# Moving the indexer queries to their rows: one stacked product per head instead of two

## The chip, the cores and the metric

The kernel runs on one core of one Trainium2 chip. The metric is the device time of one execution in microseconds (us). TensorE (PE) multiplies, VectorE (DVE) and ScalarE (ACT) do elementwise work, GpSimd (POOL) does elementwise work and issues one kind of DMA, SyncE (SP) issues the others.

## The reference, cut to what matters

Two layers of an encoder, for 512 prompt frames and 64 sample frames (576 in all) with the same weights. In each layer an indexer with 8 heads of 32 numbers scores all keys, and attention then works on the best keys only:

```
qi = rope(qi.reshape(B, T, IDX_HEADS, IDX_DIM), pos)          # 8 heads x 32
ki = rope(ki[:, :, None, :], pos)[:, :, 0]
s = einsum('thd,sd->ths', qiB, kiB) * IDX_DIM ** -0.5
score = einsum('th,ths->ts', wB, relu(s)) * IDX_HEADS ** -0.5
_, sel = top_k(score, k_sel)
```

The selection has to agree with float32, so each float32 operand of an fp32r product is held as a high part (rounded to fp32r) and a low part (what is left).

## The kernel before, in words

Activations lie transposed: 128 features on partitions, 576 frames along the free axis. A projection of 128 output columns is one `block` (line 462): 8 steps (`step`, line 440) of 6 matmuls with 288 frames each, high and low parts of weights and activations, 48 matmuls into a PSUM buffer of the tag `mm` (2 buffers). All other PSUM use has the tag `sm` (4 buffers). DVE multiplies a block's result with the norm factor `Rt` and so empties the buffer.

Each layer begins with the two blocks of the indexer's queries (`ps_q0`, `ps_q1`), 4 heads in each; the blocks u, z, gate, k, q, v and more follow in the list `ORDER`. After rope a query block `qr` has four heads of 32 rows each on the 128 partitions. The scores want each head by itself as 128 rows [high, low, high, low] against the keys' rows `KS` = [high, high, low, low], so that one product with 128 rows gives the sum of the four partial products. `qi_out` (line 644) makes this: ACT copies the whole block to `h` (the high part), DVE subtracts to `lo`, and for each of the four heads m two products with 0/1 matrices (windows of `turn_m`) place the rows of `h` and of `lo` in one PSUM buffer, 448 frames (the first 128 need no scores). Two copies, by ACT for even m and by DVE for odd m, take the result to `QS` and `QSs`. `turn_m` is 544 columns behind `KS` in one buffer: POOL clears it, DVE writes eight 32x32 identities into it (lines 668 to 675).

The order of instructions is written out while the program is built. `Plan` (line 66) keeps an estimated clock for each engine and a ready time for each piece of data. Work other than blocks is in generators: `start` queues one with a rank (0 first), and `pump` (line 231), which is called after each step of six matmuls, runs those whose condition holds at the planned time. `need(engine, data)` is true when the data are ready by the plan, for PE 0.4 us before the planned time of PE (`MARGIN`); `psum_free` is true when an `sm` buffer is free by the plan. So a generator that isn't ready lets one more step of a block go ahead of it. Each engine then runs its instructions in the order written.

What follows in the code: `ki_stack` (line 688) splits the keys on ACT and DVE, PE transposes the head weights into an `sm` buffer and DVE copies them to `wcol`; `select` (line 738) computes scores and finds the best keys on DVE; `attend` (line 1126) and `sample` (line 1146) are attention for the prompt and sample frames, on PE, DVE and ACT, between the blocks; the layer ends with 12 blocks' worth of output products.

Of the kernel before, what the change touches and what calls it, by code (L numbers as in the profile page):

```python
# [10 lines left out]
F32 = mybir.dt.float32  # L11
F32R = mybir.dt.float32r
AF = mybir.ActivationFunctionType
OP = mybir.AluOpType

P = 128
# [3 lines left out]
T = TP + TS  # L20
# [45 lines left out]
class Plan:  # L66
# [142 lines left out]
    def need(self, eng, *aps, room=None):  # L209

        now, e = self.now, self.free[eng]
        if room is not None and e - now > room:
            return False
        t = max([self.ready(x, eng) for x in aps], default=0.0)
        return t <= (now - MARGIN if eng == "pe" else max(e, now) + EPS_T)

    def start(self, gen, rank=1):
        item = [rank, len(self.todo), gen, None]
        self.todo.append(item)
        self.todo.sort(key=lambda x: x[0])  # L220
        self.step(item)
        return item
# [46 lines left out]
def encoder_step(ctx: ExitStack, tc: tile.TileContext, a: dict):  # L269
    nc = tc.nc  # L270
    plan = Plan()
    pe, act, dve, pool, dma = (Engine(plan, n, e) for n, e in (
        ("pe", nc.tensor), ("act", nc.scalar), ("dve", nc.vector), ("pool", nc.gpsimd), ("dma", nc.sync)))
    need, start = plan.need, plan.start
# [10 lines left out]
    def tmp(n=T, dtype=F32):  # L285
        return rot.tile([P, 608], dtype, name="tmp", tag="tmp", bufs=NTMP)[:, :n]

    def quart(dtype=F32):
        plan.wait("quart", NQ)
        return plan.slot("quart", NQ, rot.tile([P, 2 * T], dtype, name="quart", tag="quart", bufs=NQ), True)  # L290
# [12 lines left out]
    def ps_mm():  # L303
        return plan.slot("mm", 2, psum.tile([P, 2, 512], F32, name="mm", tag="mm", bufs=2), False)

    def ps_s(hold=False):
        return plan.slot("sm", 4, psum.tile([P, 512], F32, name="sm", tag="sm", bufs=4), hold)
# [4 lines left out]
    def psum_free(k=1):  # L312
        return plan.slots("sm", 4, k)
# [122 lines left out]
    ps = ps_s()  # L436
# [25 lines left out]
    def block(xh, xl, nk=8):  # L462
        w, i = weights()
        split_to(i + 3)
        ps = ps_mm()
        product(ps, w, xh, xl, nk)
        return ps
# [90 lines left out]
    def layer(l, x, arrive):  # L558
# [24 lines left out]
        for k in range(8 + lag[1]):  # L583
# [4 lines left out]
            if k < 8:  # L588
                c = (k % 2) * T
# [17 lines left out]
        for s in range(2):  # L607
            c = slice(s * HT, (s + 1) * HT)
# [33 lines left out]
            return sh  # L642

        def qi_out(b, qr, sh):
            h, lo = tmp(dtype=F32R), tmp(dtype=F32R)
            dve.tensor_tensor(sh, sh, SI, op=OP.mult)
            dve.tensor_tensor(qr, qr, sh, op=OP.add)

            def go():
                yield lambda: need("act", qr)  # L650
                act.copy(h, qr)
                yield lambda: need("dve", h)
                dve.tensor_tensor(lo, qr, h.bitcast(F32), op=OP.subtract)

                for m in range(4):
                    yield lambda: psum_free() and need("pe", h, lo, turn_m)
                    ps = ps_s()
                    for i, s in enumerate((h, lo)):
                        c = 32 * (1 + 4 * m - i)
                        pe.matmul(ps[:, :T - P], lhsT=turn_m[:, c:c + P], rhs=s[:, P:T], start=i == 0, stop=i == 1)  # L660
                    copy = dve.tensor_copy if m % 2 else act.copy
                    copy(QSv[:, 4 * b + m], ps[:, :3 * P])
                    copy(QSsv[:, 4 * b + m], ps[:, 3 * P:T - P])
                done.add(("qi", b))

            start(go(), 0)

        KSW = quart(F32R)
        KS, turn_m = KSW[:, :T], KSW[:, T:T + 17 * 32]
        pool.memset(turn_m.bitcast(F32), 0.0)  # L670
        for m in range(4):
            r = slice(32 * m, 32 * m + 32)
            for i in (0, 2):
                c = 32 * (1 + 4 * m + i)
                dve.tensor_copy(turn_m[r, c:c + 32], ident[r, r])
        qi_out(0, qr0, sh0)

        ko = tmp()
# [46 lines left out]
        start(ki_stack(), 1)  # L725
        qr1 = tmp()
        qi_out(1, qr1, rope(ps_q1[:, :, :HT], qr1, CI, SI))

        macc = quart()
# [614 lines left out]
        for m2 in range(4):  # L1344
            w, n = weights()
            split_to(n + 3)
            for i in range(2):
                m = 2 * m2 + i
# [3 lines left out]
                ps = ps_mm()  # L1352
                product(ps, w, oh, ol, 4, off=512 * i)
                c = slice(i * T, (i + 1) * T)
# [25 lines left out]
        for m in range(8):  # L1380
# [7 lines left out]
            ps = block(mh, ml)  # L1388
# [57 lines left out]
        for s, t0, t1, starts in ((0, 0, CUT, (0, P, CUT - P)), (1, CUT, T, (CUT, T - P))):  # L1446
            for m in (6, 7):
                w, ps = wps[m - 6]
# [21 lines left out]
    def arrive(k):  # L1470
# [3 lines left out]
        if k == 1:  # L1474
            split_first()

    x = layer(0, x, arrive)
    for l in range(1, DEPTH):
        x = layer(l, x, lambda k: None)
# [106 lines left out]
```

## Time and profile before

| what | value |
|---|---|
| time, median of 3 runs | 921.59 us (921.48 to 923.78) |
| time of the profiled execution | 922.67 us |
| its span, first to last instruction | 920.9 us |
| PE busy | 895.8 us, 97% |
| DVE busy | 669.1 us, 73% |
| ACT busy | 593.3 us, 64% |
| POOL busy | 201.7 us, 22% |
| granted TensorE clock, share of full speed | 0.994 |

The profiled execution's own time is 1.8 us over its span and 1.1 us over the median. Busy time of an engine counts an instruction from its start to its end; matmuls overlap, so the distance between their starts tells what one costs in a row of them.

### The profile page before, as it was taken

How to read it: one execution, taken by the hardware profiler on the slowest of the kernel's cores; microseconds unless marked ns; L12 is line 12 of the kernel's file. 1: busy time of each engine (PE TensorE's matmuls, PEld its weight loads, DVE VectorE, ACT ScalarE, POOL GpSimd, SP SyncE). 2: the span in 40 equal slices, each digit the busy share in tenths (PEclk: the TensorE clock that was granted, in tenths of full speed). 3: DMA queues.
4: the chain of work that ended last, by engine and by line, in shares of the span. 5: the costliest groups of instructions: out<-in, count | busy, mean ns of one | idle time of the engine just before them, and what ended most of it. 6: DMA issues, size and time to landing. Idle time of an engine off the chain costs nothing.

```text
span 920.9 us, 17399 instructions
## 1 busy us (share of the span) xinstructions
PE 895.8 (97%) x6613; PEld 882.8 (96%) x6613; DVE 669.1 (73%) x1554; ACT 593.3 (64%) x1056; POOL 201.7 (22%) x217
## 2 busy tenths in 40 slices
PE   8999999999999999999999999999999999999995
PEld 7999999998999999999999999999999999999995
DVE  6896899799896676462259779988989875755314
ACT  7456533688898975564536564446889988556652
POOL 3111211135341310112210111113443222011121
PEclk9999999999999999999999999999999999999998
DMA  7757588766465775778976666787655558648862
GB/s 266 185 135 171 115 217 202 165 165 164 114 156 138 185 197 140 200 202 232 273 184 168 166 149 160 190 203 182 162 143 130 157 123 221 189 133 222 236 145 104
DMA packets 54500, 160.97 MB, mean 175 GB/s; under 512 B 6736, under 2 KB 9040, under 8 KB 54416
## 3 DMA queue, kind: packets, MB, share of 16 engines
q0 software_dynamic: 16416, 59.78, 34.7%
q1 hardware_dynamic: 38000, 100.08, 32.5%
q8 instruction: 52, 0.85, 0.4%
q14 instruction: 32, 0.26, 0.1%
HBM read 85.37 MB, written 14.69 MB: 109 GB/s over the span
## 4 chain that ended last, share of the span: by engine, by line
PE 67%; DVE 14%; ACT 14%; issue 3%; DMA 1%; POOL 1%; SPq 0%; DVEq 0%; ACTq 0%; POOLq 0%
PE mm L263 56%; PE sm L263 11%; DVE quart L263 6%; DVE tmp L263 6%; ACT prob L263 4%; ACT whl L263 3%; ACT quart L263 2%; ACT qz L263 1%; ACT L263 1%; ACT tmp L263 1%; DVE big L263 1%; POOL tmp L263 1%; DMA raw<-in_w_dram 1%; DVE acc L263 1%; DMA prob<-in_c_v_dram 1%
## 5 line engine op out<-in xcount | busy, mean ns | idle before, releaser
L263 PE MATMUL mm<-quart,whl 128*128 128x288 f32 (+1 forms) x5568 | 780.9, 296 | 1.2 <-DVE tmp L263 1.2
L263 PEld LDWEIGHTS mm<-quart,whl 128*128 128x128 f32 x5568 | 755.2, 188 | 3.3 <-ACT quart L263 1.5
L263 POOL DMA_DIRECT2D whl<-raw x114 | 99.1, 870 | 650.4 <-ACT whl L263 435.3
L263 ACT CAST whl<-raw 128x1024 fp32r<-128x1024 f32 (+1 forms) x118 | 121.8, 1033 | 130.3 <-PE mm L263 89.4
L263 ACT ACTIVATE whl<-raw 128x1024 fp32r<-128x1024 f32 x114 | 120.5, 1057 | 0.0
L263 ACT ACTIVATE prob<-prob,stat 128x128 f32<-128x128 f32 (+3 forms) x128 | 67.5, 554 | 6.8 <-DVE stat L263 6.4
L263 DVE SCALAR_TENSOR_TENSOR quart<-prob,wcol,quart 128x256 f32<-128x256 f32 (+4 forms) x60 | 42.1, 704 | 26.4 <-ACT prob L263 25.2
L263 ACT ACTIVATE prob<-sm 128x256 f32<-128x256 f32 (+4 forms) x72 | 33.6, 481 | 38.6 <-PE sm L263 38.6
L263 DVE MATCH_REPLACE8 quart<-stat,quart 128x256 f32<-128x256 f32 (+2 forms) x96 | 51.2, 540 | 0.0
L263 DVE MAX8 stat<-quart 128x8 f32<-128x256 f32 (+2 forms) x96 | 47.4, 542 | 0.0
L263 DVE MAX8 quart<-quart 128x8 f32<-128x544 f32 x64 | 46.2, 722 | 1.2
L263 DVE MATCH_REPLACE8 quart<-quart 128x544 f32<-128x544 f32 x64 | 45.4, 709 | 0.0
L263 DVE TENSOR_TENSOR tmp<-tmp 128x576 f32<-128x576 f32 (+7 forms) x62 | 44.3, 720 | 1.3
L263 DVE TENSOR_TENSOR quart<-quart 128x576 fp32r<-128x576 f32 (+6 forms) x30 | 26.4, 881 | 21.5 <-ACT quart L263 21.0
L263 DVE TENSOR_TENSOR big<-sm,big 128x512 fp32r<-128x512 f32 (+1 forms) x64 | 28.9, 483 | 16.3 <-ACT big L263 16.1
L263 ACT CAST quart<-tmp 64x512 fp32r<-64x512 f32 (+4 forms) x44 | 24.1, 566 | 21.8 <-POOL tmp L263 11.7
L263 ACT COPY prob<-sm 64x512 f32<-64x512 f32 (+1 forms) x24 | 12.3, 514 | 39.0 <-PE sm L263 38.6
L263 PE MATMUL sm<-quart,big 128*128 128x128 f32 (+3 forms) x176 | 32.1, 291 | 1.4 <-DVE tmp L263 1.4
L263 ACT CAST big<-sm 128x512 fp32r<-128x512 f32 (+2 forms) x72 | 28.0, 434 | 7.9 <-PE sm L263 7.4
L263 DVE CUSTOM_DVE_ANT_0 prob<-sm,quart 128x512 f32<-128x512 f32 (+2 forms) x48 | 25.8, 549 | 4.8 <-PE sm L263 4.8
L263 DVE SCALAR_TENSOR_TENSOR quart<-tmp,gains,quart 128x576 fp32r<-128x576 f32 x8 | 6.6, 820 | 29.4 <-ACT quart L263 29.4
L263 DVE TENSOR_TENSOR quart<-mm,tmp 128x576 f32<-128x576 f32 (+2 forms) x10 | 6.4, 638 | 29.0 <-PE mm L263 28.9
(157 smaller groups left out, 1028.4 us busy)
## 6 DMA issues: line engine op xcount, KB each, us to landing
raw<-in_w_dram SPq DMA_DIRECT2D x116, 512.0 KB, 4.6
whl<-raw POOLq DMA_DIRECT2D x114, 512.0 KB, 4.9
mp<-tmp SPq DMA_DIRECT2D x16, 288.0 KB, 3.1
tmp<-mp SPq DMA_DIRECT2D x16, 288.0 KB, 4.8
prob<-in_c_k_dram SPq DMA_DIRECT2D x16, 256.0 KB, 5.0
prob<-in_c_v_dram SPq DMA_DIRECT2D x16, 256.0 KB, 3.8
out_o_v_dram<-quart SPq DMA_DIRECT2D x8, 320.0 KB, 4.5
quart<-in_x_dram SPq DMA_DIRECT2D x8, 288.0 KB, 6.3
```

What stands on the lines that cost most here:

```text
L263: return f(*args, **kw)
```

## The change

`qi_out` builds two operands per block instead of `h` and `lo`: `hl[e]` has the high parts of heads 2e and 2e+1 on its partitions 0 to 63 and their low parts on 64 to 127, 448 frames. ACT and DVE make each with one copy and one subtraction on 64 partitions. One product with a 0/1 matrix then moves a head's high and low rows, and `turn_m` is one 128x128 matrix for even heads and one for odd heads. The four instructions that make the operands are written out together, without a wait of the planner between a copy and its subtraction; a head's product waits for its own pair's operand.

```diff
         def qi_out(b, qr, sh):
-            h, lo = tmp(dtype=F32R), tmp(dtype=F32R)
+            hl = [tmp(dtype=F32R)[:, :T - P] for _ in range(2)]
...
             def go():
+
                 yield lambda: need("act", qr)
-                act.copy(h, qr)
-                yield lambda: need("dve", h)
-                dve.tensor_tensor(lo, qr, h.bitcast(F32), op=OP.subtract)
+                for e in range(2):
+                    src = qr[64 * e:64 * e + 64, P:T]
+                    act.copy(hl[e][0:64], src)
+                    dve.tensor_tensor(hl[e][64:128], src, hl[e][0:64].bitcast(F32), op=OP.subtract)
 
                 for m in range(4):
-                    yield lambda: psum_free() and need("pe", h, lo, turn_m)
+                    yield lambda: psum_free() and need("pe", hl[m // 2], turn_m)
                     ps = ps_s()
-                    for i, s in enumerate((h, lo)):
-                        c = 32 * (1 + 4 * m - i)
-                        pe.matmul(ps[:, :T - P], lhsT=turn_m[:, c:c + P], rhs=s[:, P:T], start=i == 0, stop=i == 1)
+                    pe.matmul(ps[:, :T - P], lhsT=turn_m[:, (m % 2) * P:(m % 2 + 1) * P], rhs=hl[m // 2], start=True, stop=True)
...
-        KS, turn_m = KSW[:, :T], KSW[:, T:T + 17 * 32]
+        KS, turn_m = KSW[:, :T], KSW[:, T:T + 2 * P]
...
-                c = 32 * (1 + 4 * m + i)
+                c = P * (m % 2) + 32 * (i + m // 2)
```

## Rows read from the trace of the kernel before

**Rows 1.** The page, busy time and share of the span of each engine.
```profile
PE 895.8 (97%) x6613; PEld 882.8 (96%) x6613; DVE 669.1 (73%) x1554; ACT 593.3 (64%) x1056; POOL 201.7 (22%) x217
```

**Rows 2.** The page, chain that ended last: share of the span by engine.
```profile
PE 67%; DVE 14%; ACT 14%; issue 3%; DMA 1%; POOL 1%; SPq 0%; DVEq 0%; ACTq 0%; POOLq 0%
```

**Rows 3.** Stretches of the span: length, then each engine's busy time, clock, DMA share, GB/s.
```profile
38.90:47.20 8.30, 8.30 (x54) 8.05 (x55) 8.02 (x20) 5.57 (x15) 0.99 (x2) 1.00 0.88 256
184.00:322.00 138.00, 135.84 (x1004) 132.77 (x1002) 115.37 (x296) 120.21 (x250) 50.51 (x47) 1.00 0.60 153
322.00:377.00 55.00, 52.97 (x401) 52.21 (x402) 36.76 (x89) 33.02 (x61) 5.17 (x6) 1.00 0.64 167
377.00:460.00 83.00, 83.00 (x624) 82.93 (x623) 32.55 (x47) 48.07 (x62) 16.57 (x17) 1.00 0.87 234
```

**Rows 4.** PE in order of time, first layer: start, length, operation, [idle before, releaser].
```profile
42.14 1.79 PE L263 MATMUL sm<-tmp,quart 128*128 128x448 f32 x8
43.77 1.76 PE L263 MATMUL mm<-quart,whl 128*128 128x288 f32 x12
45.36 1.79 PE L263 MATMUL sm<-tmp,quart 128*128 128x448 f32 x8
46.99 7.36 PE L263 MATMUL mm<-quart,whl 128*128 128x288 f32 x54
```

**Rows 5.** The same for the second layer.
```profile
488.61 1.38 PE L263 MATMUL sm<-tmp,quart 128*128 128x448 f32 x6
490.37 0.64 PE L263 MATMUL sm<-tmp,quart 128*128 128x448 f32 x2 [0.38 <-DVE wcol L263]
490.85 1.75 PE L263 MATMUL mm<-quart,whl 128*128 128x288 f32 x12
```

**Rows 6.** Groups by shape: busy us, mean ns of one, idle before.
```profile
L263 ACT CAST qz<-tmp 64x512 fp32r<-64x512 f32 x32 | 19.8, 620 | 4.0 <-DVE tmp L263 3.5
L263 ACT COPY quart<-quart 64x256 f32<-64x256 f32 x4 | 1.6, 404 | 0.1
L263 DVE TENSOR_TENSOR qzl<-tmp,qz 64x512 fp32r<-64x512 f32 x16 | 10.9, 683 | 0.3
L263 DVE TENSOR_TENSOR prob<-sm,prob 64x256 f32<-64x256 f32 x8 | 3.3, 417 | 12.4 <-ACT prob L263 12.4
L263 ACT ACT_TABLE_LOAD x17 | 21.8, 1283 | 1.0 <-PEq L1560 0.7
```

**Rows 7.** All engines in order of time, first layer: the instructions that split and read.
```profile
37.44 0.67 ACT L263 CAST tmp<-tmp 128x576 fp32r<-128x576 f32 x1 [3.96 <-DVE tmp L263]
38.65 2.20 DVE L263 TENSOR_TENSOR tmp<-tmp 128x576 f32<-128x576 f32 x3
42.41 0.54 DVE L263 TENSOR_SCALAR wcol<-sm 128x24 f32<-128x24 f32 x3
43.78 0.75 DVE L263 TENSOR_TENSOR tmp<-tmp 128x576 fp32r<-128x576 f32 x1
```

**Rows 8.** DVE in order of time, second layer.
```profile
485.93 2.20 DVE L263 TENSOR_TENSOR tmp<-tmp 128x576 f32<-128x576 f32 x3
489.69 0.54 DVE L263 TENSOR_SCALAR wcol<-sm 128x24 f32<-128x24 f32 x3
```

**Rows 9.** POOL and DVE in order of time, first layer: clearing and filling `turn_m`.
```profile
25.44 0.89 POOL L263 MEMSET quart<- 128x544 f32 x1
30.98 1.07 DVE L263 CAST quart<-ident 32x32 fp32r<-32x32 f32 x8
```

**Rows 10.** PE in order of time: two idle times between 184 and 345 us.
```profile
221.10 0.77 PE L263 MATMUL sm<-ident,tmp 128*128 128x128 f32 x5 [0.89 <-ACT tmp L263]
337.37 0.63 PE L263 MATMUL sm<-ident,quart 128*128 128x128 f32 x4 [1.20 <-DVE quart L263]
```

**Rows 11.** DVE and PE in order of time, where the first layer's attention ends.
```profile
379.39 0.29 DVE L263 TENSOR_TENSOR quart<-prob,quart 128x128 fp32r<-128x128 f32 x1 [0.86 <-ACT quart L263]
376.70 15.54 PE L263 MATMUL mm<-quart,whl 128*128 128x288 f32 x115
```

## The prediction, before the kernel was run

> **What bounds the kernel now.** I read the page's busy times first: PE is busy 97% of the span, DVE 73%, ACT 64% [rows 1]. Then the chain that ended last: PE has 67% of it, DVE and ACT 14% each [rows 2], so time taken from PE should count, unless it falls where the chain runs through the other two. Then the stretches. Where the change sits, 38.9 to 47.2 us in the first layer, PE is busy 8.30 us of 8.30 and DVE 8.02: both are full, ACT (5.57) has room [rows 3]. In the attention of that layer (184 to 322 us) PE is busy 135.84 of 138.00 us with ACT at 120.21 and DVE at 115.37; to its end at 377 us PE has 52.97 of 55.00, and in the output products 83.00 of 83.00 [rows 3]. PE has work nearly everywhere, because a generator that isn't ready lets a step of a block pass. The granted clock is 1.00 in all these stretches [rows 3], the upper of the two levels, 2.4 GHz; as the stretch stays full I cost nothing for the clock. Last I read the instructions around the change in order of time, PE first, then who feeds it.
>
> **Removed from PE.** A query block has 8 products of 448 columns, two blocks in each of two layers make 32, and the change leaves 16. Their price is the distance between starts, not their length: the eight at 42.14 are followed by the next matmul at 43.77, the eight at 45.36 by one at 46.99, 1.63 us both times, so 1.63 / 8 = 0.204 us each [rows 4]. The second layer's first group takes 488.61 to 490.85 with 0.38 us of waiting in it [rows 5]; its product itself is no dearer, so I use 0.204. Removed: 16 x 0.204 = 3.26 us. That the remaining products have other data in their rows is no cost that a row shows: shape, type and the weights of 128 columns stay.
>
> The Trainium skill, in "TensorE: Matmul & The Clock Gate", section "Back-to-back issue gap", says that in a stream of weight load and matmul pairs the spacing is set by both together, and gives about 131 ns for 512 columns. An estimate by that page is 16 x 0.131 = 2.1 us removed in place of 3.26. The trace does not agree with 131 ns: the 448 columns here are 0.204 us apart [rows 4], and I stay with the row; what the page's price would bring is a rival below.
>
> **ACT and DVE.** Four copies of 128x576 at 0.67 us and four subtractions at 0.75 us [rows 7] become eight of each on 64x448. The trace has no such shape in this place, so I take it between two: ACT needs 620 ns for 64x512 and 404 for 64x256, 0.84 ns per column, so 620 - 54 = 566 ns for 448; DVE 683 and 417 ns, 1.04 ns per column, so 683 - 67 = 617 ns [rows 6]. Half the partitions save next to nothing. One block costs ACT 2 x 0.566 - 0.67 = +0.46 us and DVE 2 x 0.617 - 0.75 = +0.48 us; in all ACT +1.9 us and DVE +1.9 us (bounds from the two sizes: 404 to 620 gives ACT +0.6 to +2.3 us, 417 to 683 gives DVE +0.3 to +2.5 us). On ACT this is hidden by its room in the stretch. On DVE it delays what stands behind: the two subtractions of the keys, the copies of `wcol`, the emptying of block u and the second block's subtractions. Emptying u 0.5 us later costs nothing, as its PSUM buffer is wanted again only after the block in progress.
>
> The planner's wait between copy and subtraction goes, so DVE, which takes its queue in order, could now stand before a subtraction until ACT has copied. It does not get there early: in the first layer ACT's copy began at 37.44 and DVE finishes the two rope instructions ahead of the subtraction (two of the three in the group at 38.65) at about 38.65 + 2 x 0.73 = 40.1 [rows 7]; two copies end at 37.44 + 1.13 = 38.6. I cost this wait at 0; without that 1.5 us of cover it would be at most one copy, 0.57 us, per block.
>
> **When are the operands ready?** First layer, first block: DVE 40.1 + 1.23 = 41.3, PE asks at 42.14 [rows 4]: in time by 0.8 us. Second block: its subtraction began at 43.78 [rows 7], now 0.48 later, so the pair is ready at 44.9 and 45.5. PE, with its second group shifted as below, asks for them at 45.4 and 45.8. In time, by only 0.3 us for the second.
>
> **A wait that grows.** Four `sm` buffers serve four heads, and one of them holds the head weights until DVE has copied them to `wcol`. In the second layer the fourth head already waits for that: `wcol` ends at 489.69 + 0.54 = 490.23 [rows 8], the matmuls go on at 490.37 [rows 5]. With half the products PE asks 0.6 us sooner, and DVE is done 0.48 us later, at 490.71. By the code the planner then finds no free buffer and puts one step of six matmuls (half of 45.36 - 43.77, 0.80 us [rows 4]) ahead of the fourth head. PE asks at 488.61 + 3 x 0.204 + 0.80 = 490.02 and starts at 490.71 + 0.14 = 490.85: 0.83 us idle in place of 0.38, +0.45. In the first layer `wcol` ends at 42.41 + 0.54 + 0.48 = 43.43 [rows 7], so 43.57 against PE at 42.14 + 0.61 + 0.80 = 43.55: 0.02. Together +0.5. If no step comes between it is 1.25 + 0.82 = 2.1 us; if two do, the 0.38 of now goes as well. Bounds -0.4 to +2.1; I take +0.5. Behind the waiting matmul only PE's own steps stand, and DVE and ACT have work.
>
> **POOL.** It clears 256 columns in place of 544. The clearing ended at 25.44 + 0.89 = 26.33, DVE's first use is at 30.98 [rows 9]: 4.6 us of cover, worth nothing. The eight identities stay, as do the number of `tmp` buffers and all DMAs.
>
> **Sum.** -3.26 + 0.5 = -2.8 us. The profiled execution took 922.67 us, 1.8 over its span of 920.9, so 919.9 for one like it; against the median of 921.59 it is 918.8 us. Does the gain last to the end? In each layer PE would reach the attention 1.4 us earlier. Attention ends on PE with a stream of 115 matmuls from 376.70; the last operand for the output products is written at 379.39 + 0.29 = 379.7 [rows 11], while PE works on the last block for some 6.4 us (48 matmuls at 0.133 us, from 1.59 / 12). That is over 3 us of slack: 1.4 us fit in.
>
> **Rivals.**
> The attention is paced by ACT and DVE, and PE just waits longer there. For: the chain's 28% on these two [rows 2] and waits such as 0.89 us for ACT and 1.20 us for DVE [rows 10]. Against: PE idles only 2.16 us in 138. Price: the whole gain; 921.6, up to 923.5 if DVE's 1.9 us came on top.
>
> Slower: everything after the change is written in a new order, since planned times shift. If the gates' sigmoids and the exponentials then alternate once more in each layer, ACT loads its tables two more times each, 4 x 1.28 us [rows 6] = 5.1 us. If PE waits for ACT in that place, as it does at 221 us [rows 10], its own saving is lost too: 921.6 + 5.1 = 926.7. It decides only if both pairs land on such a wait; by half of it, 2.6 us, the result would be no visible change. Against: ACT has 138.0 - 120.2 = 17.8 us free there [rows 3].
>
> The new order loses waits: the two of [rows 10] come to 2.1 us and each layer has its own; without most of them 2.8 + 3 = 5.8 us are gained, 915.8.
>
> The change doesn't bring what it says: matmuls are removed that cost less than their distance. At the skill's price it is -2.1 + 0.5 = -1.6 us, 920.0.
>
> **How the numbers follow.** A measurement of this kernel can tell about 0.3%, 2.8 us, from no change, and my forecast lies on that edge. Forecast case 0.60 (918.0 to 920.4 by the bounds of the wait: 3.26 + 0.4 and 3.26 - 2.1), split 0.33 faster and 0.27 within; paced by others 0.14, within; slower order 0.14; waits lost 0.09, faster; cheap products 0.03, within. Faster 0.42, same 0.44, slower 0.14. The range that leaves out about 2 in 10, most of the slower order and the far end of the lost waits, is 916.0 to 924.0.
>
> **What would show it.** 16 products of 448 columns in groups 0.2 us apart, with 3.3 us less of them; eight copies near 0.57 us and eight subtractions near 0.62 us; a step of six matmuls between the third and fourth head of the first block; 0.8 us idle before that head in the second layer; after that PE's idle per layer as now. I am wrong if the stretches from 184 to 377 us take longer by as much as was saved before them, if table loads are more than 17, or if subtractions that read two partition ranges take much over 0.7 us.

## The result, and the profile after

| what | before | after |
|---|---|---|
| median, 6 runs each | 922.78 us (921.48 to 923.78) | 927.63 us (927.10 to 929.28) |
| profiled execution, its span | 922.67, 920.9 us | 927.59, 925.8 us |

The ratio of after to before is 1.0055, 95% interval 1.0045 to 1.0065: slower by 4.9 us, where 2.8 us of gain were forecast. The page shows less work on PE and nearly the same share [rows 1], and PE has more of the chain [rows 2]:

```profile
PE 894.0 (97%) x6597; PEld 881.2 (95%) x6597; DVE 676.4 (73%) x1558; ACT 594.8 (64%) x1060; POOL 201.2 (22%) x217
...
PE 74%; DVE 11%; ACT 11%; issue 2%; DMA 1%; POOL 1%; SPq 0%; DVEq 0%; POOLq 0%; ACTq 0%
```

Around the change, PE after in order of time, both layers (the lines that answer to [rows 4, 5]):

```profile
41.52 0.77 PE L263 MATMUL sm<-tmp,quart 128*128 128x448 f32 x3
42.14 0.96 PE L263 MATMUL mm<-quart,whl 128*128 128x288 f32 x6
43.18 0.44 PE L263 MATMUL sm<-tmp,quart 128*128 128x448 f32 x1
43.46 1.75 PE L263 MATMUL mm<-quart,whl 128*128 128x288 f32 x12
...
46.03 0.47 PE L263 MATMUL sm<-tmp,quart 128*128 128x448 f32 x1 [0.41 <-DVE quart L263]
...
490.93 0.45 PE L263 MATMUL sm<-tmp,quart 128*128 128x448 f32 x1 [0.91 <-DVE wcol L263]
```

The step of six matmuls stands between the third and fourth head, and the fourth waits 0.91 us for `wcol` in layer 1. By shape, after, the new copies and subtractions, and one group that the change doesn't touch (busy us, mean ns of one):

```profile
L263 DVE TENSOR_TENSOR quart<-quart 64x544 f32<-64x544 f32 x4 | 8.9, 2229 | 1.7 <-ACT quart L263 1.6
...
L263 DVE TENSOR_TENSOR tmp<-tmp 64x448 fp32r<-64x448 f32 x8 | 5.0, 619 | 0.2
...
L263 ACT CAST tmp<-tmp 64x448 fp32r<-64x448 f32 x8 | 4.5, 560 | 8.6 <-DVE tmp L263 8.5
```

The first group is two additions per layer that join two parts of the sample's scores ahead of its selection. The kernel before took 2.9 us for it, not 8.9:

```profile
L263 DVE TENSOR_TENSOR quart<-quart 64x544 f32<-64x544 f32 x4 | 2.9, 720 | 0.2
```

Where did the time go? I compared the same event in both traces. The matmul stream behind the first layer's attention begins at 376.60 after and 376.70 before. But after was 0.62 us ahead when the first query block's products came near (the 24 matmuls in front of them start at 38.25 against 38.87), so from there to the attention's end the first layer took 0.5 us longer, with the 1.6 us of its products saved. Most of the loss is in the second layer (layer 1). PE before:

```profile
642.83 0.40 PE L263 MATMUL sm<-quart,qz 128*128 128x512 f32 x1
770.70 0.33 PE L263 MATMUL sm<-ident,prob 128*128 128x128 f32 x1 [0.81 <-ACT prob L263]
785.39 0.63 PE L263 MATMUL sm<-ident,quart 128*128 128x128 f32 x4 [1.20 <-DVE quart L263]
824.72 15.54 PE L263 MATMUL mm<-quart,whl 128*128 128x288 f32 x115
```

and after:

```profile
644.93 1.33 PE L263 MATMUL sm<-ident,tmp 128*128 128x128 f32 x5 [2.92 <-ACT tmp L263]
645.91 0.78 PE L263 MATMUL sm<-quart,qz 128*128 128x512 f32 x1
766.12 0.44 PE L263 MATMUL sm<-ident,prob 128*128 128x128 f32 x2 [1.02 <-ACT prob L263]
774.39 0.40 PE L263 MATMUL sm<-ident,prob 128*128 128x128 f32 x1 [2.00 <-ACT prob L263]
790.61 0.63 PE L263 MATMUL sm<-ident,quart 128*128 128x128 f32 x4 [1.20 <-DVE quart L263]
829.95 10.34 PE L263 MATMUL mm<-quart,whl 128*128 128x288 f32 x76
```

The attention's first product is 3.1 us late (645.91 against 642.83), the last unit 3.7 (774.39 against 770.70), the sample's first transposes 5.2 (790.61 against 785.39), and so it stays. Behind both long waits the granted clock is at the lower level, 1.2 GHz, for some 3 us (stretches of after; the clock is the third figure from the right):

```profile
645.00:648.00 3.00, 3.00 (x11) 2.81 (x12) 1.94 (x6) 3.00 (x7) 0.69 (x1) 0.50 0.00 0
775.00:778.00 3.00, 3.00 (x14) 2.91 (x13) 1.05 (x2) 1.82 (x3) 0.00 (x0) 0.51 0.84 203
```

Why does the attention start late? DVE before, just ahead of it, in order of time:

```profile
627.42 1.47 DVE L263 TENSOR_TENSOR quart<-quart 64x544 f32<-64x544 f32 x2
...
630.40 0.81 DVE L263 STREAM_SHUFFLE tmp<-mm 128x576 f32<-128x576 f32 x1
...
636.39 0.82 DVE L263 STREAM_SHUFFLE tmp<-mm 128x576 f32<-128x576 f32 x1
```

DVE after:

```profile
628.68 0.83 DVE L263 STREAM_SHUFFLE tmp<-mm 128x576 f32<-128x576 f32 x1
...
630.73 4.48 DVE L263 TENSOR_TENSOR quart<-quart 64x544 f32<-64x544 f32 x2 [0.59 <-ACT quart L263]
...
638.31 0.81 DVE L263 STREAM_SHUFFLE tmp<-mm 128x576 f32<-128x576 f32 x1
```

POOL after:

```profile
630.99 1.76 POOL L263 TENSOR_TENSOR tmp<-tmp,St 128x576 f32<-128x576 f32 x1
632.83 1.80 POOL L263 TENSOR_TENSOR tmp<-tmp 128x576 f32<-128x576 f32 x1
```

The first shuffle is the key rope's, the last the first query rope's, from which ACT makes the operands `qz`. Behind these casts ACT copies the value block (at 644.25 after, 642.48 before), and for that copy PE's first value transposes wait. Before, the additions ran ahead of the key rope. After, they stand behind it, beside POOL's half of that rope, and take 4.48 us in place of 1.47; two selection rounds (MAX8, MATCH_REPLACE8) follow, and the query rope starts 1.9 us later although its block ended no later on PE.

### The profile page after: what moved, and what is told of

It is laid out like the page before. It is cut to its first block, busy times and chain, and to the rows that moved or that the text cites. A ratio compares the mean times of both kernels' runs of the same rounds, so it can differ in the third digit from the quotient of the medians.

```text
span 925.8 us, 17394 instructions
## 1 busy us (share of the span) xinstructions
PE 894.0 (97%) x6597; PEld 881.2 (95%) x6597; DVE 676.4 (73%) x1558; ACT 594.8 (64%) x1060; POOL 201.2 (22%) x217
## 3 DMA queue, kind: packets, MB, share of 16 engines
HBM read 85.37 MB, written 14.69 MB: 108 GB/s over the span
## 4 chain that ended last, share of the span: by engine, by line
PE 74%; DVE 11%; ACT 11%; issue 2%; DMA 1%; POOL 1%; SPq 0%; DVEq 0%; POOLq 0%; ACTq 0%
PE mm L263 63%; PE sm L263 12%; DVE quart L263 5%; DVE tmp L263 4%; ACT whl L263 3%; ACT prob L263 3%; ACT quart L263 2%; ACT qz L263 1%; DMA raw<-in_w_dram 1%; ACT tmp L263 1%; POOL tmp L263 1%; ACT big L263 1%; DVE acc L263 1%; DVE big L263 0%; ACT L263 0%
## 5 line engine op out<-in xcount | busy, mean ns | idle before, releaser
L263 ACT ACTIVATE prob<-prob,stat 128x512 f32<-128x512 f32 (+3 forms) x128 | 68.0, 555 | 4.3 <-DVE stat L263 3.9
L263 DVE TENSOR_TENSOR quart<-quart 128x576 fp32r<-128x576 f32 (+6 forms) x30 | 32.4, 1081 | 14.4 <-ACT quart L263 13.1
L263 PE MATMUL sm<-ident,prob 128*128 128x128 f32 x160 | 24.9, 277 | 5.9 <-ACT prob L263 4.4
L263 DVE TENSOR_TENSOR tmp<-mm,tmp 128x576 f32<-128x576 f32 x28 | 21.0, 751 | 12.2 <-PE mm L263 11.9
```

Source lines behind the costliest of these rows:

```text
L263: return f(*args, **kw)
```

## The experiments

Times are compared by the ratio to the kernel before on the same chip, in brackets its 95% interval; after stands at 1.0055. Traces of the same instructions reach layer 1 up to 1.2 us apart: its second query rope starts at 484.42 us in after and at 485.65 in `casts_behind_last_exp`, which is the same up to there. Where that matters, times in layer 1 are counted from this rope (484.57 in before).

**1. Operands or order?** `new_ops_old_order` writes the changed instructions in the order of before on every engine: the planner is charged for the old ones.

```diff
-                    act.copy(hl[e][0:64], src)
+                plan.run("act", "copy", (h, qr), {})
+                for e in range(2):
+                    nc.scalar.copy(hl[e][0:64], src[e])
...
+                        plan.run("pe", "matmul", ...)   # twice
+                    nc.tensor.matmul(..., rhs=hl[m // 2], ...)
```

> The changed kernel's instructions (stacked operands, 16 products) written in exactly the order of the kernel before: the planner is charged for the old ones. Theory 'order': the loss came from the new order of all later work, so here the change's own value shows, 3.3 us less of products less some 1 to 2 us of growing waits for the wcol buffer: 1 to 2.5 us faster than before, about 921 us. Rival 'operands': the stacked instructions themselves are dearer than thought (subtractions over two partition ranges, buffers freed late); then most of the loss stays with the old order: 926 to 928 us.

Measured: 922.75 us, ratio 0.9993 [0.9984, 1.0001]. The loss is gone, but so is the gain; PE's idle times at the products say why:

```profile
43.32 0.44 PE L666 MATMUL sm<-tmp,quart 128*128 128x448 f32 x1 [0.91 <-DVE wcol L263]
46.25 0.67 PE L666 MATMUL sm<-tmp,quart 128*128 128x448 f32 x2 [0.48 <-ACT quart L263]
...
491.05 0.45 PE L666 MATMUL sm<-tmp,quart 128*128 128x448 f32 x1 [1.71 <-DVE wcol L263]
493.97 0.68 PE L666 MATMUL sm<-tmp,quart 128*128 128x448 f32 x2 [0.48 <-ACT quart L263]
```

3.58 us, against 0.38 before: the 3.26 us saved are waited away.

`old_ops_new_order` is the reverse: the planner is charged for the new instructions, and the old ones are issued.

```diff
+                    plan.run("act", "copy", (hl[e][0:64], src), {})
+                    plan.run("dve", "tensor_tensor", (hl[e][64:128], ...), ...)
+                nc.scalar.copy(h, qr)
+                nc.vector.tensor_tensor(lo, qr, h.bitcast(F32), op=OP.subtract)
...
+                    plan.run("pe", "matmul", ...)   # once, two are issued
```

> The kernel before's instructions (h and lo, 32 products) written in exactly the order of the changed kernel. Theory 'order': as slow as the changed kernel or slower by the products, 927 to 931 us. Rival 'operands': as fast as the kernel before, 921 to 924 us.

Measured: 927.85 us, 1.0045 [1.0033, 1.0057], with the additions and waits of after:

```profile
645.26 1.33 PE L263 MATMUL sm<-ident,tmp 128*128 128x128 f32 x5 [2.93 <-ACT tmp L263]
766.42 0.44 PE L263 MATMUL sm<-ident,prob 128*128 128x128 f32 x2 [1.02 <-ACT prob L263]
774.69 0.37 PE L263 MATMUL sm<-ident,prob 128*128 128x128 f32 x1 [2.02 <-ACT prob L263]
```

So the order makes the loss. The stacked operands add nothing that can be told apart (1.0055 and 1.0045, with overlapping intervals), and in this order the 16 products that they save bring no visible gain either.

**2. Is it this order, or any other?** `old_ops_third_order` is before, with only the planner's PE clock set back after each query block.

```diff
+                plan.free["pe"] -= 0.82
                 done.add(("qi", b))
```

> The kernel before with all its instructions, only the planner's estimate of PE's clock set back by 0.82 us after each of the four query blocks, so that the later work is written in a third order. Theory 'order is chance': the time moves by some us in either direction with no instruction changed, 917 to 930 us and not within 1 us of the kernel before. Rival 'only this order': 921.5 to 924 us.

Measured: 928.5 us, 1.0047 [1.0034, 1.0059]. The same pattern, now in the first layer:

```profile
197.44 0.77 PE L263 MATMUL sm<-ident,tmp 128*128 128x128 f32 x5 [2.90 <-ACT tmp L263]
...
326.90 0.33 PE L263 MATMUL sm<-ident,prob 128*128 128x128 f32 x1 [2.02 <-ACT prob L263]
```

0.82 us in the planner's clock at each of four blocks, with no instruction changed, costs as much as the change. One more order doesn't tell what an order costs on average; whether the order of before is an unusually good one is not tested.

**3. The lower clock.** `fill_idle` is after with dummy products, whose results are overwritten, put into the two waits of layer 1.

```diff
+                for _ in range(12 if l == 1 and p == 0 else 0):
+                    nc.tensor.matmul(pv[:, :P], lhsT=ident, rhs=ident, start=True, stop=True)
...
+            for _ in range(7 if (l, p, e, j) == (1, 3, 1, 0) else 0):
```

> The changed kernel with dummy products in the two longest idle times of PE in the second layer (12 ahead of the first v transposes, 7 ahead of the last head's probability transposes); they compute nothing that is used. Theory 'clock': the granted clock was 0.50 for 3 to 4 us after each of these two idle times, which costs about 1.8 us each; with PE kept busy it stays at 1.00 and the time falls to 924 to 925 us. Rival: the idle time alone is the loss; no change, 927 to 928 us, or slower if the dummies get in the way.

Measured: 926.26 us, 1.0030 [1.0019, 1.0041]. The granted clock is 1.00 behind both places (644 to 650 and 774 to 779 us). Layer 1 gained 1.5 us, all of it behind the second: at the first, PE waits 0.69 us for ACT soon behind it (648.87), and the attention is no earlier at 766 us (281.7 us behind that layer's second query rope, as in after). The trace of `casts_behind_last_exp` (experiment 5) says the same: there the clock stayed at 1.00 behind a first wait of 2.93 us, and this event again comes 281.7 us behind the rope. So the lower clock is a part of the loss behind the second wait, and none that reaches 766 us behind the first.

**4. The late start: rounds or additions?** `rounds_behind_rope` is after, with DVE's two selection rounds of layer 1 held back behind the first query rope.

```diff
+                for k in range(8):
+                    step(ps, w, xh, xl, k, 8)
+                    if k == HOLD: holding[0] = True   # max, match_replace go to `held`
...
                 dve.tensor_tensor(qr, qr, sh, op=OP.add)
+                holding[0] = False
+                while held: ...   # issued here
```

> The changed kernel with one move on VectorE alone, in layer 1: the two selection rounds (MAX8 and MATCH_REPLACE8, 2 x 1.5 us) that stand between the sample's two 64x544 additions and the first query rope go behind that rope. Theory 'the attention of layer 1 starts late because VectorE is still at its selection when the first query block ends': the rope's shuffle starts at 635.6 to 636.0 in place of 638.31, the first query product at 643.0 to 643.5 in place of 645.91, TensorE's wait at 644.93 falls from 2.92 to under 1.3 us and no half clock follows it; all later events of layer 1 come 2.4 to 3 us earlier and the time is 924.6 to 925.4. Rival 'the half clock behind the wait and the ACT order later in the layer make the loss': the first wait shrinks, but the stretch to 766 us takes longer by as much, time 927 to 928.

Measured: 925.36 us, 1.0034 [1.0021, 1.0046]. The rope starts at 635.43 and the wait is 0.77 us, but of the 2 us gained there 1 is left at 766 us (765.27 against 766.12, in a trace that reached layer 1 0.18 us later): the held rounds now stand ahead of the subtractions that make `qzl`, and two new waits of 0.83 and 0.72 us follow. The rest of the gain is the clock behind the second wait, which was not lowered in this execution:

```profile
642.96 0.77 PE L263 MATMUL sm<-ident,tmp 128*128 128x128 f32 x5 [0.77 <-ACT tmp L263]
644.79 0.51 PE L263 MATMUL sm<-quart,qzl 128*128 128x512 f32 x1 [0.83 <-DVE qzl L263]
667.25 0.55 PE L263 MATMUL sm<-ident,prob 128*128 128x128 f32 x3 [0.72 <-ACT prob L263]
765.27 0.44 PE L263 MATMUL sm<-ident,prob 128*128 128x128 f32 x2 [1.02 <-ACT prob L263]
773.55 0.33 PE L263 MATMUL sm<-ident,prob 128*128 128x128 f32 x1 [2.02 <-ACT prob L263]
788.24 0.63 PE L263 MATMUL sm<-ident,quart 128*128 128x128 f32 x4 [1.20 <-DVE quart L263]
```

`adds_ahead_of_key_rope` is after, with DVE's two additions put ahead of the key rope, in both layers.

```diff
+                behind("dve", "stream_shuffle", (halves(sh), ps[:, :, :HT], SHUF), {})
+                behind("dve", "tensor_tensor", (halves(kr), ...), {"op": OP.mult})
...      # kept in `late`, with POOL's two, until the additions are out
             dve.tensor_tensor(s2[64:128], ...)
+            for eng, op, args, kw in late: ...
```

> The changed kernel with one move on VectorE and none elsewhere, in both layers: the two 64x544 additions of the sample go ahead of the first key rope's shuffle and product, so that they no longer run beside GpSimd's two 128x576 operations of that rope. In the traces so far the two additions took 1.47 us where GpSimd was idle (the kernel before, both layers) and 4.48 us where they ran beside these operations (the changed kernel, both layers). Theory 'VectorE's additions, both inputs in SBUF, stand still while GpSimd reads SBUF': they take 1.47 us again, GpSimd's two start 3 us later, the first query rope in layer 1 starts at 636.4 to 636.9 in place of 638.31, the wait of 2.92 us falls to 0.9 to 1.6 us, time 925.3 to 926.4. Rival 'the additions are long for another reason (their inputs' place, the wait for ACT)': 4.4 to 4.5 us again and the time 927.3 to 929, as the key rope is now behind them.

Measured: 925.77 us, 1.0037 [1.0023, 1.0051]. The additions take 1.47 us again:

```profile
630.64 1.47 DVE L263 TENSOR_TENSOR quart<-quart 64x544 f32<-64x544 f32 x2 [1.97 <-ACT quart L263]
...
636.72 0.82 DVE L263 STREAM_SHUFFLE tmp<-mm 128x576 f32<-128x576 f32 x1
...
639.29 1.73 DVE L263 TENSOR_TENSOR tmp<-tmp 128x576 f32<-128x576 f32 x1
```

The rope starts 1.6 us earlier, but its last addition now falls beside POOL's subtractions (637.35 to 640.4) and takes 1.73 us where it took 0.76 in after. The wait is 2.34 us, not the 0.9 to 1.6 expected: the stall has moved as much as gone.

`adds_behind_key_rope` is before with the opposite move.

```diff
-            dve.tensor_tensor(s2[0:64], ...)
+            behind("tensor_tensor", (s2[0:64], ...), ...)   # and the first round
...
             sh = rope(ps[:, :, :HT], kr, Ct[0], St)
+            if p == 0: ...   # issued here
```

> The kernel before with the opposite move, on VectorE alone, in both layers: the two 64x544 additions of the sample, with the first selection round, go behind the first key rope's shuffle and product, and so beside GpSimd's two operations of that rope. Theory 'VectorE's additions stand still while GpSimd reads SBUF, and this late start is the loss': the additions take 4.3 to 4.5 us in place of 1.47, the first query rope of layer 1 starts 2.5 to 3.2 us later than 636.39, TensorE waits 2.5 to 3 us for ACT at the first value transposes with a half clock behind it, and with nothing of the change in it the kernel is slower by 2 to 5 us, 925 to 928. Rival 'the additions are not the cause': 1.47 us and 922.5 to 923.3.

Measured: 924.21 us, 1.0020 [1.0011, 1.0028]: slower, but less than I expected, and not by the stall. DVE:

```profile
630.82 1.46 DVE L1000 TENSOR_TENSOR quart<-quart 64x544 f32<-64x544 f32 x2
...
638.54 0.82 DVE L263 STREAM_SHUFFLE tmp<-mm 128x576 f32<-128x576 f32 x1
```

POOL:

```profile
632.41 1.77 POOL L263 TENSOR_TENSOR tmp<-tmp,St 128x576 f32<-128x576 f32 x1
```

Here the additions didn't wait for ACT, and POOL's pair began when they were done. Being behind the rope is not enough: in after they also wait 0.59 us for ACT and begin within 0.3 us of POOL's pair (630.73 against 630.99), and then POOL's operations end first. The query rope starts 1.4 us late, counted from the layer's second query rope (2.2 by the clock of the trace), by one more round ahead of it, and PE waits 0.65 us.

**5. The second wait.** `casts_behind_last_exp` is after, with ACT's two casts of a weight piece put behind the exponential of the last unit.

```diff
+            if before_exp[0]: held_split.append(real)
...
             act.activation(lm[:, :n], lm[:, :n], AF.Exp, ...)
+            if (p, e, j) == (3, 1, 0) and l == 1: ...   # issued here
```

> The changed kernel with one move on ScalarE alone, in layer 1: the two casts of a weight piece (1.05 us each, at 769.89 and 770.84 in the changed kernel's trace) that stand ahead of the table load and the exponential of the attention's last unit go behind that exponential; nothing else changes. Theory 'of the 5.2 us lost in layer 1 about 2 us lie here: TensorE waits 2.00 us for that unit, and the half clock that follows costs 1.5 us more (774.39 to 790.61 us took 16.22 us, the same stretch of before 14.69)': the wait falls from 2.00 to under 0.4 us, no half clock follows it, and the time is 924.3 to 926 us. Rival 'the casts are needed as early as they stand': TensorE waits as long a little later for the weight piece (a wait <-ACT whl or POOL whl of 1 to 2 us at 775 to 780), time 927 to 928.

Measured: 926.57 us, 1.0032 [1.0021, 1.0044]. The wait shrank only to 1.55 us (ACT still has other work ahead of the table load), but the stretch behind it ran at full clock, 14.70 us in place of 16.22:

```profile
646.19 0.77 PE L263 MATMUL sm<-ident,tmp 128*128 128x128 f32 x5 [2.93 <-ACT tmp L263]
...
775.19 0.33 PE L263 MATMUL sm<-ident,prob 128*128 128x128 f32 x1 [1.55 <-ACT prob L263]
789.89 0.63 PE L263 MATMUL sm<-ident,quart 128*128 128x128 f32 x4 [1.20 <-DVE quart L263]
```

`both_moves` has this and the held rounds, the two diffs above together.

> The changed kernel with both moves in layer 1: the two selection rounds behind the first query rope (alone: 925.36 us), and the weight casts behind the last unit's exponential. If these two places are the loss, their gains add, as they lie behind one another on the same path: the first gained 0.85 us by 766 us and lost the half clock behind the second wait, the second wait is 2.02 us there. Time 923.3 to 924.3. What is then still missing to before (0.5 to 1.5 us) would be VectorE's 3 us of standing still beside GpSimd, which no move of order gives back. If the time stays at 925 or more, the last unit's wait was not on the path.

Measured: 924.55 us, 1.0013 [1.0004, 1.0022]. By the ratios the gains add: 0.0021 and 0.0023 alone, 0.0042 together, 3.9 us of the 5.1 that after loses, with 1.2 us left. The traces don't bear out that sum. From layer 1's second query rope to the sample's first transposes, before takes 300.82 us and after 306.19, 5.4 more; the rounds alone give back 2.6 of that, the casts alone 2.0 and both 3.1 (303.14), because the 1.5 us of the clock behind the second wait are in both single gains and can be had only once. By either count more than half of the loss lies in these two places of layer 1. In what is left, PE still waits for ACT where the attention ends:

```profile
766.01 0.44 PE L263 MATMUL sm<-ident,prob 128*128 128x128 f32 x2 [1.02 <-ACT prob L263]
773.81 0.33 PE L263 MATMUL sm<-ident,prob 128*128 128x128 f32 x1 [1.55 <-ACT prob L263]
```

That is 2.57 us, where before has the one wait of 0.81 at 770.70. DVE's stall is still in this kernel too, and its share isn't shown.

**6. What is a product worth?** `double_products` is before, with the second block's products issued twice.

```diff
                         pe.matmul(..., rhs=s[:, P:T], start=i == 0, stop=i == 1)
+                    if b:
+                        for i, s in enumerate((h, lo)):
+                            nc.tensor.matmul(...)   # the same again
```

> The kernel before, its order and its instructions, but each of the second query block's products is issued twice (8 more per layer, 16 in all; by the duration of one in its trace, 0.204 us, 3.26 us more of TensorE). Theory 'TensorE sets the time wherever nothing is waiting, so that one product is worth 0.2 us': 3 to 3.5 us slower than before, 925.6 to 926.2 beside 922.6. Rival 'the attention behind it is paced by ACT and DVE, so that a product is worth little': TensorE's waits in the attention shrink by as much, and the time is 0 to 1.2 us over before.

Measured: 926.67 us, 1.0036 [1.0023, 1.0049]: 3.5 us for 16 products by the medians, 0.22 each. PE sets the time here.

`products_behind_steps` is `new_ops_old_order` with some products, and the copies that empty them, one or two steps later on PE.

```diff
+                    n = (0, 0, 0, 1 + l)[m] if b == 0 else (0, 0, 1, 1)[m]
+                    if n: later.append([n, real])   # issued after n steps
```

> The changed instructions (16 products, casts and subtractions per 64 rows) in the order of before on all engines, except on TensorE: there the fourth head's product of the first query block goes one step (layer 0) or two steps (layer 1) later, and the third and fourth head's of the second block one step later, so that none of them has to wait for its operands; the two copies that empty each product go with it. In the same instructions without this move TensorE waited 0.91 + 0.48 us in layer 0 and 1.71 + 0.48 us in layer 1 at these products, 3.58 us, against 0.38 us before. Theory 'TensorE sets the time, and the waits ate the saving': with the waits gone (sum of the idles at the six-matmul steps under 0.6 us) the 3.26 us less of products come out, 919.5 to 920.3 us beside 922.8 for before (3 us faster). Rival 'the attention is paced by ACT and DVE': the products are shorter, but waits of the same size grow behind them in the attention (226 to 322 and 680 to 770 us), time within 0.7 us of before, 922.2 to 923.5.

Measured: 921.04 us, 0.9986 [0.9977, 0.9995], between the two theories. One wait was left in layer 1:

```profile
491.97 0.64 PE L679 MATMUL sm<-tmp,quart 128*128 128x448 f32 x2 [1.13 <-DVE tmp L666]
```

`products_two_steps` takes that one away as well:

```diff
-... else (0, 0, 1, 1)[m]
+... else (2 * l, 2 * l, 1 + 2 * l, 1 + 2 * l)[m]
```

> The changed instructions in the order of before with the products moved behind steps, as in the run that gave 921.04 us, and in layer 1 all four heads of the second block two steps later than there. In that run TensorE still waited 1.13 us at 491.97 for VectorE's subtraction. Theory 'that wait is on the path': it falls under 0.3 us and the time is 0.6 to 1.1 us less, 919.9 to 920.5. Rival 'it is hidden by what VectorE and ScalarE do behind it': another wait of that size appears before 670 us, time 920.7 to 921.5.

Measured: 921.00 us, 0.9977 [0.9967, 0.9987]: 2.1 us faster than before, the best of all. The wait is gone, but from a matmul of that layer's second block (485.86 here) to the end of its attention the trace gained 0.16 us (485.86 to 823.64, against 485.45 to 823.39): the wait was mostly hidden by what VectorE and ScalarE do behind it (PE now waits 0.35 us for ACT at 522.43, and at 558.05 it waits 0.87 us for DVE in place of 0.61). So with the order held and the waits taken out, 1.3 and 2.1 us of the 3.26 are gained by the ratios, the second with an interval from 1.2 to 3.0.

## Why the prediction was wrong

- **Local terms: right.** 16 products fewer at 0.2 us; copies 560 ns (566 forecast), subtractions 619 (617); the step of six; the growing wait 0.91 us (0.83). Not forecast were waits of 0.41 us at 46.03 and 0.27 at 494.64, for the emptying of buffers by DVE and ACT. And the second layer's products are not shown to be "no dearer" by [rows 5]: less the wait they stand 1.86 us / 8 = 0.23 apart; experiment 6 measured 0.22.
- **The step that failed** is "Does the gain last to the end? [...] That is over 3 us of slack: 1.4 us fit in." It takes the instructions behind the change to stand in the order of before and asks only whether 1.4 us fit at the layer's end. The planner wrote another order in both layers, and that makes the result (experiment 1: 1.0045 for the order, 0.9993 for the instructions). What the runs show in its place: in layer 1 DVE's additions fall beside POOL's rope and stand still for 3 us, the query rope starts late with two rounds ahead of it, and the attention starts 3.1 us late; and ACT has casts and more ahead of the last unit's exponential, so that PE waits 2.00 us there in place of 0.81, with 1.5 us lost by the clock behind it. Work moved out of both places gave back 3.9 of 5.1 us by the ratios, 3.1 of 5.4 in the traces. How the rest of the late start reaches the layer's end is not shown: of the 2 us won back at the start only 1 arrived.
- **The clock**: "as the stretch stays full I cost nothing" failed where the new waits are, 100 us behind the change and more.
- **The slower rival** had the side and nearly the size (926.7), but not the mechanism: there are 17 table loads, as before [rows 6]. I gave it 0.14 and priced one accident; experiment 2 shows that another small shift of the plan costs the same, so the loss by a new order deserved more.
- **"Paced by ACT and DVE"** was right in part: by the measured ratios a third or more of the saved time doesn't arrive with the order held (the interval leaves 0.2 to 2.1 us), while added products cost their full price. A price for more PE work is not one for less.
- **The growing wait at +0.5 us** holds only in the planner's own new order; in the old order the same instructions wait 3.58 us.

What stays open: the 1.2 us (by the ratios; 2.3 in the traces) that the two moves don't give back, and the share of DVE's stall in the loss. The stall alone doesn't make the loss: the additions take 4.50 us in the first layer of after too, where only the 1.6 us saved there and 0.5 more are lost, and no run takes the stall away without moving it elsewhere.

## What to carry to other kernels

Where a planner writes the order from estimated times, a change of 1 us in the plan can rewrite everything behind it: first run the new instructions in the old order and the old in the new, so that the two effects are told apart. Before pricing what is removed, list which engine is full next to it; the time removed comes back as waits unless what feeds it is moved as well. And look for pairs of DVE and POOL operations with SBUF inputs that a new order could bring side by side.

## What the runs showed of the hardware

DVE's two 64x544 additions, both inputs in SBUF, took 1.46 to 1.47 us where POOL's two 128x576 operations came later, and 4.47 to 4.50 in every trace where the two pairs began within 0.3 us of each other (both layers of after, of the kernels in its order and of `old_ops_third_order`). In those, DVE is recorded as the first to begin, by 0.26 us, yet its pair ends 0.6 us behind POOL's (635.21 against 634.63 in after). The query rope's last addition, 128x576, took 0.76 us in after and 1.73 and 1.78 beside POOL's subtractions in `adds_ahead_of_key_rope` and `rounds_behind_rope`. DVE's MAX8, MATCH_REPLACE8 and its operations that read PSUM were no slower beside POOL (0.72, 0.71 and 0.74 us). The Trainium skill, in "SBUF — State Buffer", section "SBUF: two separate sides", says that a DVE operation with two SBUF inputs and a GpSimd operation that reads SBUF lock each other out, and that the one which starts first goes ahead for its whole length. These traces agree with the first part, by the 3.0 us above; the second they don't show, as the operation recorded first is the one that waited.

The granted clock after a wait of PE differed between traces: a wait of 2.92 us was followed by 0.50 in after, and one of 2.93 at the same place by 1.00 in `casts_behind_last_exp`; one of 2.02 us by 0.51 in `old_ops_new_order` and, at the same place, by 1.00 in `rounds_behind_rope`. Behind the second place the lower clock made the stretch to the sample's first transposes 16.22 us in place of 14.69, 1.5 us more; behind the first it cost nothing that was left at 766 us.
